# Two more pairs of up-projection tiles by seven products, with part of the operand work on GpSimd

## The chip, the cores and the metric

One core of a Trainium2 chip runs the kernel. Its engines have a queue of instructions each and wait for each other by semaphores: TensorE (PE; its weight loads are shown as PEld), VectorE (DVE), ScalarE (ACT), GpSimd (POOL) and SyncE (SP), which here only issues DMAs. The metric is the device time of one execution in microseconds (us): the median of the runs of a kernel. One further execution is profiled; the trace and its page are of that one.

## The reference, cut to what matters

The reference is one step of a decoder layer for 512 prompt positions and 8 samples of 4 positions, 544 rows in all: a mixer (recurrent branch, windowed attention, gates, output projection), and then a feed-forward network with a short convolution. The change lies in the second half:

```python
x = x + _rmsnorm(m, norm_mix_post[l])
u = _rmsnorm(x, norm_ffn_pre[l]) @ w_up              # 1024 -> 8192 columns
u, conv_state = _causal_dwconv(u, ffn_prev, ...)     # width 3 over positions
val, gate = jnp.split(u, 2, axis=-1)
f = (gelu(gate) * val) @ w_down                      # 4096 -> 1024
x = x + _rmsnorm(f, norm_ffn_post[l])
```

Everything is float32.

## The kernel before, in words

**Products.** Each float32 operand is split into a high part (a rounded copy, by ACT) and a low part (the operand less the high part, by DVE), and a product of two operands is three matmul passes: high by high, high by low, low by high. The up projection's 64 tiles of 128 columns are taken as 32 pairs: tile j of the values with tile 32 + j of the gates. The 544 rows are two halves of 272 (a = 0 and a = 1), and the 1024 rows of the weights two halves of 512 (u = 0 and u = 1). A "product" (`product`, L1522) is one half of the weights of a tile against one half of the rows: 4 blocks of 128 by three passes, 12 matmuls of 272 columns.

**Three ways for a pair.** Pairs 0 to 3 (`early`, L1372) are done plainly, 8 products each, first all 16 products of the first half of the rows, then all 16 of the second half. Pairs 4 and 5 (`PLAIN = 6`) are plain too, 8 products each, both halves of the rows together. Pairs 6 to 31 are done by a seven-product scheme (`pair`, L1640): the products a11, a12, p2, p3, p1, p4, a22 with the operands b11, b21, t2, t3, t1, b22, t4 (the table `XOF`). The weights of p2, p3, p1 and p4 are sums of quarters of the pair's two tiles, the operands t1 to t4 are sums of quarters of the normalised rows, and what the products give is added and subtracted again on the way out of PSUM (`taken`, `u4_c22`, `c11`, `c12`, `c21`; their copies `e` lie in the pool "parts", 5 buffers).

**Raw weights.** A tile of `w_up` is loaded by SP as 512 KB into one of 5 buffers ("raw"), in the order of use; a buffer is free again when the last split of its contents is done. A pair by eight products needs two raw tiles (`raw_up__...` of j and of 32 + j); a pair by seven products needs three, since the tile j is loaded a second time (`raw_up_s`) as the place in which the sums for p2 and p4 are made. `sums` (L1457) makes them in two parts: part 0 is one add by DVE, p3 = the second copy of tile j + the tile 32 + j; part 1 is one add by DVE in the tile 32 + j and two adding DMAs issued by GpSimd, the second of which waits for the first.

**Units, and how far ahead they are split.** A unit is what one (high, low) pair of split weights serves: for plain tiles two products, for the seven-product scheme one, for the down projection two halves. The list `units` has the 16 units of the early pairs first (0 to 15), in the order of the 16 products of the first half. `ahead(n)` (L1487) puts into the queues the loads up to unit n + 10, the high parts (ACT) and the low parts (DVE) up to n, and then every `sums` whose place has come: part 0 of a pair when n + 1 reaches the index of its p2 in the list less 4, part 1 one later (`SUMS = (4, 3)`, L1484 and L1499). While the 16 early products of the first half are written out, the product number k (from 0) calls `ahead(k + 5)`, up to 16; the first four of the second half call `ahead` with 17, 18, 19 and 20; after that the place moves with each unit used.

**Order.** The queues of PE, ACT and DVE in this stretch are written out by hand: instructions run in the order in which the program names them. A product is followed by a slot (`slot`, L1591): first what is due of earlier tiles (copies out of PSUM, the taps of the convolution, gelu and gate product: `tap`, `glu`), then `ahead`, then the generators that run beside the products (in the early products of the first half `ahead` comes after the generators). GpSimd's and SP's queues are put in order by a planner.

**The normalised rows.** `norm_chain(1, ...)` (L1232) runs beside the products, half a tick (one slot) for each `yield 0.5`. It makes the second half of the normalised rows: in slots 12 and 13 the tiles `h2t` and their splits b12 and b22, which product 16 and product 17 are the first to use; in slots 14 and 15 it forms t2 and the sum that becomes t1 in `h2f`; in 16 and 17 the sums that become t4 (two adds by DVE, 544 columns each); in 18 and 19 the high and the low part of t2; in 20 and 21 the sums that become t3 (two subtractions by DVE in `h2t`). Then it rests for `TX = 4` ticks (8 slots) and splits t3, t1 and t4 in slots 30 to 40, the high part and two slots later the low part, all low parts by DVE. The tiles `h2t` lie in a pool that is given up when the first tile of "parts" or "psums" (where the raw p3 of a pair lies) is asked for; the new pools lie over it.

**Down halves.** `plan` (L1372 to L1394) puts the halves of the down projection (12 matmuls of 256 or 288 columns) in between, once the pairs that they need are through: for plain pairs after the last product of a tile, two for a pair; for pairs by seven products after the products that `LAST_PLACES` names, by default four.

Of the kernel before, what the change touches and what calls it, by code (L numbers as in the profile page):

```python
# [11 lines left out]
F32 = mybir.dt.float32  # L12
F32R = mybir.dt.float32r
AF = mybir.ActivationFunctionType
ALU = mybir.AluOpType
AX = mybir.AxisListType

P = 128
# [40 lines left out]
HP = 150  # L59
NSTART = (1, 0.5)  # L60
EARLY = 4
PLAIN = 6
FB = (0.5,)
LASTS = 6
HELD = 5
TY = 1
TX = 4
DNS = 5
LAST_PLACES = {29: ('p3', 'p1', 'a22'), 30: ('p3', 'p1', 'a22'), 31: ('p1', 'a22')}
FIRST = 5  # L70
ATTN = (8, 10, 12, 14, 16, 18, 20, 22, 24, 26, 29, 32, 35, 38, 40, 42)
SAMPLE = (41, 46)
# [49 lines left out]
def hawk_step(ctx, tc, I, O):  # L122
    nc = tc.nc
    act, dve, pool, pe = nc.scalar, nc.vector, nc.gpsimd, nc.tensor
# [16 lines left out]
    def S(name, dt=F32):  # L141
        return sp.tile([P, SLOT], dt, tag="s", name=name)

    def T(name, dt=F32):
        return tp.tile([P, FLAT + 4], dt, tag="t", name=name)
# [13 lines left out]
    def f32(ap):  # L159
        return ap.bitcast(F32)  # L160
# [4 lines left out]
    def sub(out, a, b):  # L165
        dve.tensor_tensor(out=out, in0=a, in1=b, op=ALU.subtract)  # L166
# [4 lines left out]
    def add(out, a, b):  # L171
        dve.tensor_tensor(out=out, in0=a, in1=b, op=ALU.add)  # L172
# [984 lines left out]
    def total(accs, n, nm):  # L1157

        ps = PX("pst_" + nm)
        for z, acc in enumerate(accs):  # L1160
            mm(ps[:, :n], ones, acc[:, :n], z == 0, z == len(accs) - 1)
        return ps

    def root_table(ps, n, nm):

        y, w = (T(f"{x}_{nm}")[:, :n] for x in ("ry", "rw"))
        act.activation(y, ps[:, :n], AF.Abs_reciprocal_sqrt, scale=1.0 / D, bias=epst)
        act.activation(w, y, AF.Square, scale=1.0 / 32.0)
        return y, w
# [30 lines left out]
    def part_pool(which):  # L1200

        if not parts:
            trans.close()
            parts["e"] = ctx.enter_context(tc.tile_pool(name="parts", bufs=E_BUFS))
            parts["p"] = ctx.enter_context(tc.tile_pool(name="psums", bufs=2))
        return parts[which]
# [6 lines left out]
    def operand(nm, k, j):  # L1213

        if (nm, k // 2) not in B:
            B[nm, k // 2] = [S(f"{nm}{x}{k // 2}", F32R) for x in "HL"]
        return B[nm, k // 2][j][:, (k % 2) * HN:(k % 2 + 1) * HN]

    def operand2(nm, k2, j):

        operand(nm, 2 * k2, j)
        return B[nm, k2][j][:, 0:2 * HN]
# [9 lines left out]
    def norm_chain(a, acc):  # L1232
        lo, hi = HALF2[a]
        n = hi - lo
        with tc.high_priority(offset=HP):
            ps = total([acc], n, f"m{a}")
        yield YS[a]
        with tc.high_priority(offset=HP):
            yw = root_table(ps, n, f"m{a}")
            if a:  # L1240
                yield 0.5
            rep = root_newton(ps, n, *yw)
            acc2 = T(f"accx{a}")
            sq = {}

            def x1_(c):
                return x1[c][:, lo:hi]

            for c in range(0 if a else 8):
                m_ = mt[c][:, lo:hi]  # L1250
                stt(m_, m_, pvn[:, G_POST + c:G_POST + c + 1], rep[:, :n], ALU.mult, ALU.mult)
                pool.tensor_tensor(out=x1_(c), in0=x1_(c), in1=m_, op=ALU.add)
                sq_sum(acc2, x1_(c), n, c == 0, f"x{a}_{c}")
            for g in range(6 if a else 0):
                for c in range(2 * g, 2 * g + 2) if g < 4 else ():
                    m_ = mt[c][:, lo:hi]
                    stt(m_, m_, pvn[:, G_POST + c:G_POST + c + 1], rep[:, :n], ALU.mult, ALU.mult)
                    pool.tensor_tensor(out=x1_(c), in0=x1_(c), in1=m_, op=ALU.add)
                for c in range(2 * g - 3, 2 * g - 1) if 1 <= g < 6 else ():
                    if 0 <= c < 8:  # L1260
                        sq[c] = acc2 if c == 0 else T(f"sq_x{a}_{c}")
                        act.activation(sq[c][:, :n], x1_(c), AF.Square)
                for c in ((), (), (), (), (1, 2, 3), (4, 5, 6, 7))[g]:
                    add(acc2[:, :n], acc2[:, :n], sq[c][:, :n])
                yield 0.5
        yield NORM_TICKS[a]
        with tc.high_priority(offset=HP):
            ps = total([acc2], n, f"f{a}")
        yield YS[a]
        with tc.high_priority(offset=HP):  # L1270
            yw = root_table(ps, n, f"f{a}")
            if a:
                yield 0.5
            rep = root_newton(ps, n, *yw)

            def normed(c, dst):
                stt(dst, x1[c][:, lo:hi], pvn[:, G_FPRE + c:G_FPRE + c + 1], rep[:, :n], ALU.mult, ALU.mult)

            def first(k2):
                return h2f[k2][:, 0:2 * HN]  # L1280

            if a == 0:
                for k2 in range(5):
                    if k2 < 4:
                        for c in (2 * k2, 2 * k2 + 1):
                            normed(c, h2_half0(c))
                        act.activation(operand2(("b11", "b21")[k2 // 2], k2 % 2, 0), first(k2), AF.Copy)
                    if k2:
                        o = [operand2(("b11", "b21")[(k2 - 1) // 2], (k2 - 1) % 2, j) for j in range(2)]
                        sub(o[1], first(k2 - 1), f32(o[0]))  # L1290
                return
            n2 = {}

            def second(k2):
                return n2[k2]

            def high(nm, src):
                for k in range(2):
                    act.activation(operand2(nm, k, 0), src(k), AF.Copy)

            def low(nm, src):
                for k in range(2):
                    sub(operand2(nm, k, 1), src(k), f32(operand2(nm, k, 0)))

            for k2 in range(5):
                if k2 < 4:
                    n2[k2] = npool.tile([P, 2 * HN], F32, name=f"h2t{k2}")
                    for z in range(2):
                        normed(2 * k2 + z, n2[k2][:, z * HN:(z + 1) * HN])
                    act.activation(operand2(("b12", "b22")[k2 // 2], k2 % 2, 0), n2[k2], AF.Copy)  # L1310
                if k2:
                    o = [operand2(("b12", "b22")[(k2 - 1) // 2], (k2 - 1) % 2, j) for j in range(2)]
                    sub(o[1], n2[k2 - 1], f32(o[0]))
                if k2 in (2, 4):
                    yield 0.5
            for c in range(8):
                nc.sync.dma_start(out=x1d[c], in_=x1[c][:, 0:NT])
            t2 = [T(f"t2_{k}")[:, 0:2 * HN] for k in range(2)]
            for k in range(2):
                sub(first(k), first(k), second(k))  # L1320
                stt(t2[k], first(k), -1.0, second(2 + k), ALU.mult, ALU.subtract)
                yield 0.5
            for k in range(2):
                add(first(2 + k), first(2 + k), t2[k])
                yield 0.5
            high("t2", lambda k: t2[k])
            yield 0.5
            low("t2", lambda k: t2[k])
            yield 0.5
            for k in range(2):  # L1330
                sub(second(k), second(k), second(2 + k))
                yield 0.5
            yield TX
            for nm, src in (("t3", second), ("t1", first), ("t4", lambda k: first(2 + k))):
                high(nm, src)
                yield TY
                low(nm, src)
                yield TY

    def out_done(c, acc):  # L1340
# [36 lines left out]
    for p_ in range(EARLY, 32):  # L1377
        if p_ < PLAIN:
            todo_ = [("q", j, u, a) for j in (p_, 32 + p_) for u in range(2) for a in range(2)]
            places = [x for x in todo_ if x[2] == x[3] == 1]  # L1380
        else:
            todo_ = [("s", p_, nm) for nm in (XOF if p_ < 31 else ENDS)]
            places = [x for x in todo_ if x[2] in LAST_PLACES.get(p_, ("a12", "p3", "p1", "a22"))]
        for x in todo_:
# [15 lines left out]
    raws, usplit, used = {}, {}, [0, 0, 0]  # L1400
# [56 lines left out]
    def sums(p_, part):  # L1457
        w = {nm: source(("s", p_, nm)) for nm in ("p1", "p2", "p4", "a22")}
        if part == 0:
            raws["p3", p_] = part_pool("p").tile([P, 4, P], F32, tag="p", name=f"p3_{p_}")  # L1460
            add(raws["p3", p_], w["p2"], w["p1"])
        else:
            add(w["p1"], w["p1"], w["a22"])
            pool.dma_start(out=w["p2"], in_=w["p1"], accum_op=ALU.add)
            pool.dma_start(out=w["p4"], in_=w["p2"], accum_op=ALU.add)  # L1465
# [532 lines left out]
```

## Time and profile before

| what | before |
|---|---|
| median of 3 runs | 974.34 us (974.23 to 974.61) |
| the profiled execution, its own time | 973.95 us |
| its span | 972.2 us |
| PE busy | 963.0 us, 99% of the span, 7634 matmuls |
| DVE busy | 756.3 us, 78% |
| ACT busy | 553.9 us, 57% |
| POOL busy | 167.9 us, 17% |
| granted PE clock | 0.999 |

The profile's time axis starts with the span; the execution's own time is 1.75 us more than the span. In rows of the timeline the columns are start, length in us, engine, line, operation, what is written and read, how many instructions are merged, and in brackets how long the engine idled before and for whom. Lengths of neighbouring instructions overlap a little: 128x512 DVE operations of 0.69 us start 0.60 us apart when they are back to back. In rows of stretches (windows), the columns are the length of the stretch, the busy time and instructions of each engine, the granted PE clock, the share of the 16 DMA engines and GB/s.

### The profile page before, as it was taken

What the parts mean: (1) busy time and instruction counts of PE and PEld (TensorE: products, weight loads), DVE (VectorE), ACT (ScalarE), POOL (GpSimd) and SP (SyncE); (2) the same over time, 40 slices, a digit from 0 to 9 for tenths busy, and PEclk for the clock granted to TensorE, in tenths of its full rate; (3) what the DMA queues carried; (4) which work ended last, traced back from release to release, by engine and by line L of the source; (5) the groups of instructions that cost most, each with busy time, mean ns of one, the idle gap of its engine ahead of it and who ended that gap; (6) DMA issues with size and microseconds to landing.
All of it is one profiled execution on the core that took longest, in us unless ns stands there. A gap on an engine that the chain in (4) does not pass through costs nothing.

```text
span 972.2 us, 20023 instructions
## 1 busy us (share of the span) xinstructions
PE 963.0 (99%) x7634; PEld 955.2 (98%) x7634; DVE 756.3 (78%) x1599; ACT 553.9 (57%) x1349; POOL 167.9 (17%) x282
## 2 busy tenths in 40 slices
PE   9999999999999999999999999999999999999997
PEld 8999999999999999999999999999999999999996
DVE  5777888857858555599967888787888888888875
ACT  6544443467476425566767665655555555656653
POOL 2242000003406330230010111111011101020024
PEclk9999999999999999999999999999999999999999
DMA  7775535532334547135157575857576766668612
GB/s 229 236 213 180 151 89 147 162 93 87 108 110 128 179 115 189 52 121 186 45 117 182 128 198 123 192 130 181 136 181 157 171 155 156 170 145 219 201 31 92
DMA packets 234203, 143.07 MB, mean 147 GB/s; under 512 B 25012, under 2 KB 218940, under 8 KB 234076
## 3 DMA queue, kind: packets, MB, share of 16 engines
q1 hardware_dynamic: 224300, 120.21, 41.8%
q0 software_dynamic: 9696, 19.42, 11.8%
q10 hardware_dynamic: 112, 2.17, 0.6%
q8 instruction: 60, 0.98, 0.4%
q14 instruction: 35, 0.29, 0.1%
HBM read 115.59 MB, written 15.17 MB: 134 GB/s over the span
## 4 chain that ended last, share of the span: by engine, by line
PE 94%; DVE 3%; ACT 1%; issue 0%; DMA 0%; POOL 0%; SPq 0%; DVEq 0%; ACTq 0%; POOLq 0%
PE pmin L163 20%; PE pmdn L163 19%; PE pux L1527 16%; PE puy L1527 8%; PE pq L1527 6%; PE pmlo L163 5%; PE pmao L163 5%; PE pmout L163 4%; PE puz L1527 4%; PE pg L163 1%; PE pvp L163 1%; PE psc L163 1%; PE ptok L163 1%; DVE wl_e L166 0%; DMA pt<-pd 0%
## 5 line engine op out<-in xcount | busy, mean ns | idle before, releaser
L163 PE MATMUL pmin<-hH,wh_in 128*128 128x256 f32 (+1 forms) x568 | 164.0, 291 | 0.0
L163 PE MATMUL pmin<-hL,wh_in 128*128 128x256 f32 (+1 forms) x568 | 162.4, 288 | 0.0
L163 PE MATMUL pmin<-hH,wl_in 128*128 128x256 f32 (+1 forms) x568 | 159.1, 288 | 0.0
L163 PE MATMUL pmdn<-fH,wh_dn 128*128 128x256 f32 (+1 forms) x448 | 129.2, 288 | 0.0
L163 PE MATMUL pmdn<-fH,wl_dn 128*128 128x256 f32 (+1 forms) x448 | 129.0, 288 | 0.0
L163 PE MATMUL pmdn<-fL,wh_dn 128*128 128x256 f32 (+1 forms) x448 | 128.9, 288 | 0.0
L163 PEld LDWEIGHTS pmin<-hH,wh_in 128*128 128x128 f32 x568 | 107.2, 189 | 1.2 <-issue 1.0
L163 PEld LDWEIGHTS pmin<-hL,wh_in 128*128 128x128 f32 x568 | 107.2, 189 | 0.1
L163 PEld LDWEIGHTS pmin<-hH,wl_in 128*128 128x128 f32 x568 | 104.7, 188 | 0.2 <-issue 0.2
L175 DVE SCALAR_TENSOR_TENSOR uc<-u,fv,uc 128x560 f32<-128x560 f32 x128 | 102.0, 797 | 1.7 <-ACT uc L1558 1.1
L163 PEld LDWEIGHTS pmdn<-fH,wl_dn 128*128 128x128 f32 x448 | 84.4, 188 | 0.0
L163 PEld LDWEIGHTS pmdn<-fL,wh_dn 128*128 128x128 f32 x448 | 84.3, 188 | 0.1
L163 PEld LDWEIGHTS pmdn<-fH,wh_dn 128*128 128x128 f32 x448 | 84.2, 188 | 0.1
L1655 ACT COPY u<-pux 128x272 f32<-128x272 f32 x52 | 20.1, 387 | 86.0 <-PE pux L1527 86.0
L166 DVE TENSOR_TENSOR u<-puy,u 128x240 f32<-128x240 f32 (+2 forms) x78 | 24.6, 344 | 49.6 <-PE puy L1527 32.5
L172 DVE TENSOR_TENSOR ft<-ft,pmdn 128x256 f32<-128x256 f32 (+1 forms) x104 | 45.1, 434 | 16.7 <-PE pmdn L163 16.7
L281 ACT ACTIVATE wh_in<-raw_in 128x512 fp32r<-128x512 f32 x70 | 42.2, 625 | 19.0 <-issue 10.6
L288 DVE TENSOR_TENSOR wl_in<-raw_in,wh_in 128x512 fp32r<-128x512 f32 x70 | 47.8, 693 | 1.0 <-ACT wh_in L281 1.0
L1558 ACT ACTIVATE uc<-u,fv 128x560 f32<-128x560 f32 x64 | 48.2, 755 | 0.0
L779 ACT ACTIVATE s<-s,st 128x256 f32<-128x256 f32 (+1 forms) x32 | 15.2, 475 | 53.0 <-DVE st L776 42.5
L166 DVE TENSOR_TENSOR wl_dn<-raw_dn,wh_dn 128x512 fp32r<-128x512 f32 x56 | 38.3, 685 | 3.6 <-ACT wh_dn L1476 3.6
L1465 POOL DMA_DIRECT2D raw_up_s<-raw_up_s x26 | 22.4, 861 | 93.2 <-DMA raw_up_s<-raw_up__11237 5.5
(743 smaller groups left out, 3374.9 us busy)
## 6 DMA issues: line engine op xcount, KB each, us to landing
raw_in<-in_w_in_dram SPq DMA_DIRECT2D x35, 512.0 KB
raw_dn<-in_w_down_dram SPq DMA_DIRECT2D x56, 256.0 KB
raw_up_s<-in_w_up_dram SPq DMA_DIRECT2D x25, 512.0 KB
raw_up_s<-raw_up_s POOLq DMA_DIRECT2D x26, 256.0 KB, 4.3
raw_ao<-in_w_attn_o_dram SPq DMA_DIRECT2D x8, 512.0 KB
raw_lo<-in_w_lru_o_dram SPq DMA_DIRECT2D x8, 512.0 KB
raw_out<-in_w_out_dram SPq DMA_DIRECT2D x8, 512.0 KB
pd<-pb SPq DMA_DIRECT2D x12, 256.0 KB
```

The costliest lines, as they stand in the source:

```text
L163: pe.matmul(out, l, r, start=start, stop=stop)
L166: dve.tensor_tensor(out=out, in0=a, in1=b, op=ALU.subtract)
L172: dve.tensor_tensor(out=out, in0=a, in1=b, op=ALU.add)
L175: dve.scalar_tensor_tensor(out=out, in0=a, scalar=s_, in1=b, op0=op0, op1=op1)
L281: act.activation(hl[0], raw, AF.Copy)
L288: (eng or dve).tensor_tensor(out=hl[1], in0=raw, in1=f32(hl[0]), op=ALU.subtract)
L779: act.activation(s3[:, j, :], s3[:, j, :], AF.Exp, bias=ng[:, j:j + 1], accum_out=sm[:, j:j + 1])
L1465: pool.dma_start(out=w["p4"], in_=w["p2"], accum_op=ALU.add)
L1527: pe.matmul(ps[:, :HN], w, x, start=start and k == 0 and i == 0, stop=stop and k == 3 and i == 2, skip_group_check=True)
L1558: act.activation(yt[j][:, 0:FLATU], u[:, 0:FLATU], AF.Copy, scale=fv[:, j:j + 1])
L1655: act.copy(e[nm_], z)
```

## The change

Pairs 4 and 5 are no longer plain but done by the seven-product scheme, with two down halves each as before (after p1 and a22). The raw p3 of pair 4 is put into a general slot, not into the pool "psums". In `norm_chain` the two subtractions for t3 and the two adds for t4 go from DVE to GpSimd and stand in slot 16; t2 is split in slots 17 and 18; the rest is half a tick; then t3, t4 and t1 are split in this order in slots 19 to 29, the low parts of t3 and t4 (two instructions each) by GpSimd and that of t1 by DVE.

```diff
-PLAIN = 6
+PLAIN = 4
...
-TX = 4
+TX = 0.5
...
-LAST_PLACES = {29: ('p3', 'p1', 'a22'), 30: ('p3', 'p1', 'a22'), 31: ('p1', 'a22')}
+LAST_PLACES = {4: ('p1', 'a22'), 5: ('p1', 'a22'), 29: ('p3', 'p1', 'a22'), 30: ('p3', 'p1', 'a22'), 31: ('p1', 'a22')}
...
-            def low(nm, src):
+            def low(nm, src, eng=dve):
                 for k in range(2):
-                    sub(operand2(nm, k, 1), src(k), f32(operand2(nm, k, 0)))
+                    eng.tensor_tensor(out=operand2(nm, k, 1), in0=src(k), in1=f32(operand2(nm, k, 0)), op=ALU.subtract)
...
             for k in range(2):
-                add(first(2 + k), first(2 + k), t2[k])
-                yield 0.5
+                pool.tensor_tensor(out=second(k), in0=second(k), in1=second(2 + k), op=ALU.subtract)
+            for k in range(2):
+                pool.tensor_tensor(out=first(2 + k), in0=first(2 + k), in1=t2[k], op=ALU.add)
+            yield 0.5
             high("t2", lambda k: t2[k])
             yield 0.5
             low("t2", lambda k: t2[k])
-            yield 0.5
-            for k in range(2):
-                sub(second(k), second(k), second(2 + k))
-                yield 0.5
             yield TX
-            for nm, src in (("t3", second), ("t1", first), ("t4", lambda k: first(2 + k))):
+            for nm, src, eng in (("t3", second, pool), ("t4", lambda k: first(2 + k), pool), ("t1", first, dve)):
                 high(nm, src)
                 yield TY
-                low(nm, src)
+                low(nm, src, eng)
                 yield TY
...
         if part == 0:
-            raws["p3", p_] = part_pool("p").tile([P, 4, P], F32, tag="p", name=f"p3_{p_}")
+            if p_ == PLAIN:
+                raws["p3", p_] = S(f"p3_{p_}")[:, 0:512].rearrange("p (k n) -> p k n", k=4)
+            else:
+                raws["p3", p_] = part_pool("p").tile([P, 4, P], F32, tag="p", name=f"p3_{p_}")
             add(raws["p3", p_], w["p2"], w["p1"])
```

## The prediction

> **What bounds the kernel now.** I read the page's busy table first, then the chain that ended last, then stretches around the edit, then the queues in order of time.
>
> ```profile
> PE 963.0 (99%) x7634; PEld 955.2 (98%) x7634; DVE 756.3 (78%) x1599; ACT 553.9 (57%) x1349; POOL 167.9 (17%) x282
> 417.40:436.30 18.90, 18.40 (x140) 17.58 (x139) 17.54 (x33) 13.15 (x29) 7.71 (x8) 1.00 0.43 137
> 436.30:447.00 10.70, 10.70 (x88) 10.70 (x87) 10.43 (x21) 6.15 (x13) 0.00 (x0) 1.00 0.96 301
> 447.00:468.00 21.00, 21.00 (x169) 21.00 (x169) 19.11 (x39) 15.80 (x52) 0.00 (x0) 1.00 0.28 85
> 468.00:498.00 30.00, 30.00 (x242) 30.00 (x241) 23.75 (x42) 21.25 (x59) 1.81 (x2) 1.00 0.35 90
> 414.32 1.72 DVE h2f L175 x4
> 436.32 49.67 PE pq L1527 x396
> 485.99 4.43 PE pmdn L163 x36
> 490.42 6.04 PE pq L1527 x48
> ```
>
> TensorE sets the time: it is busy 99%, and the chain runs through it without a break from 436.32 on. So a removed product is worth its length, and a microsecond for which TensorE is made to wait is lost. But where the edit lies DVE is nearly as full: busy 17.54 of 18.90 us, 10.43 of 10.70, 19.11 of 21.00. The last links of the chain that aren't TensorE are DVE's normalised rows (414.32). The engine that the edit loads is the one without room.
>
> The chain gives the clock of what follows. 396 matmuls are 33 products in 49.67 us, 1.505 us each. They end with the twelfth plain product of pairs 4 and 5, so they are products 11 to 43 of the stretch; product k starts at 436.32 + (k - 11) x 1.505: product 16, the first to use b12, at 443.85, product 17 (b22) at 445.35, product 32 (the first of pair 4) at 467.93.
>
> **1. What is removed.** Two pairs by 7 instead of 8 products: -2 x 1.505 = **-3.0 us**, whole, as nothing else fills TensorE. The number of down halves stays (two a pair before, two after).
>
> **2. The sums of pair 4 move up, into DVE's fullest place.** This is the step that I think decides.
>
> ```profile
> 481.27 0.69 DVE L166 TENSOR_TENSOR wl_dn<-raw_dn,wh_dn 128x512 fp32r<-128x512 f32 x1
> 481.88 0.68 DVE L172 TENSOR_TENSOR p<-raw_up_s,raw_up__6410 128x512 f32<-128x512 f32 x1
> 484.35 0.69 DVE L172 TENSOR_TENSOR raw_up__6410<-raw_up__6410 128x512 f32<-128x512 f32 x1
> 435.46 0.68 DVE L166 TENSOR_TENSOR wl_e<-raw_up__5779,wh_e 128x512 fp32r<-128x512 f32 x1
> 436.06 0.68 DVE L166 TENSOR_TENSOR wl_e<-raw_up__5883,wh_e 128x512 fp32r<-128x512 f32 x1
> 436.66 0.69 DVE L166 TENSOR_TENSOR wl_e<-raw_up__5918,wh_e 128x512 fp32r<-128x512 f32 x1
> 437.92 0.69 DVE L166 TENSOR_TENSOR wl_e<-raw_up__5918,wh_e 128x512 fp32r<-128x512 f32 x1
> 438.53 0.43 DVE L175 SCALAR_TENSOR_TENSOR rw_f<-pst_f,rw_f 128x272 f32<-128x272 f32 x1
> 444.11 1.53 DVE L166 TENSOR_TENSOR b22L<-h2t,b22H 128x544 fp32r<-128x544 f32 x2
> 433.72 0.38 SPq L1440 DMA_DIRECT2D raw_up__6065<-in_w_up_dram  x1
> 436.17 0.38 SPq L1440 DMA_DIRECT2D raw_up__6115<-in_w_up_dram  x1
> 436.64 1.51 SPq L1317 DMA_DIRECT2D x1d<-x  x2
> ```
>
> Before, the first pair by seven products is pair 6, and its p2 is unit 28; the rule n + 1 = 28 - 4 puts part 0 of its sums behind the low part of unit 22, and there it is, 481.88 behind 481.27. After, p2 of pair 4 is unit 18, so part 0 comes at n = 13, behind the low part of unit 12 (436.06), and part 1 one low part later. At 436.66 DVE thus comes to an add that reads the second copy of tile 4. This copy is the eleventh raw tile; there are five buffers, so it takes that of the sixth, which is free when unit 11 is split (435.46 + 0.68). Before, the eleventh load is raw_up__6115, issued at 436.17, right behind that. So the add is reached half a microsecond after its load is issued. How long does a load take?
>
> ```profile
> 875.64 0.37 SPq L1440 DMA_DIRECT2D raw_up_s<-in_w_up_dram  x1
> 882.61 0.69 DVE L172 TENSOR_TENSOR p<-raw_up_s,raw_up__12376 128x512 f32<-128x512 f32 x1 [0.94 <-DMA raw_up_s<-in_w_up_dram]
> 485.64 0.94 POOL L1464 DMA_DIRECT2D raw_up_s<-raw_up__6410  x1 [53.81 <-DVE raw_up__6410 L172]
> 489.26 0.87 POOL L1465 DMA_DIRECT2D raw_up_s<-raw_up_s  x1 [2.68 <-DMA raw_up_s<-raw_up__6410]
> ```
>
> Pair 30's same add waited for its load and started 6.97 us after the issue. The lower end is the 256 KB transfer that GpSimd waited for, 3.62 us. So the copy lands between 439.8 and 443.1. In between: the DMA engines are 96% busy here at 301 GB/s, with raw_up__6065 (512 KB) and an x1d store (272 KB) queued before; with the copy's own 512 KB that is 1.33 MB or 4.4 us from 436.3, and the two stores of 436.64 share in it. I take 441.2.
>
> Behind the waiting add in DVE's queue stand the low parts of units 13 to 15, and rw_f, h2t, b12 and b22, which TensorE needs at products 13 to 17. All come later by the wait (441.2 - 436.66 = 4.5) and the two adds (0.60 each, back to back): 5.75 us. The room: the second b22 low part ends at 445.64, and product 17 needs it in its eighth matmul, at 445.35 + 7 x 0.125 = 446.23; so 0.6 is hidden. **+5.1 us** (3.75 to 7.05 for the two ends).
>
> **3. DVE in slots 14 to 36.** Edits that go together: four operand sums and t3's and t4's low parts leave DVE, t1's low part comes ahead of pair 4, pair 5's p3 add comes into slot 19, and from slot 33 every product needs a low part of its own.
>
> ```profile
> 448.36 0.72 DVE L172 TENSOR_TENSOR h2f<-h2f,t 128x544 f32<-128x544 f32 x1
> 452.05 1.35 DVE L166 TENSOR_TENSOR t2L<-t,t2H 128x544 fp32r<-128x544 f32 x2
> 454.88 1.35 DVE L166 TENSOR_TENSOR h2t<-h2t,h2t 128x544 f32<-128x544 f32 x2
> 469.62 0.91 DVE L175 SCALAR_TENSOR_TENSOR z<-uc,fv,uc 128x512 f32<-128x512 f32 x2 [0.83 <-ACT uc L1569]
> 470.45 1.64 DVE L175 SCALAR_TENSOR_TENSOR uc<-u,fv,uc 128x560 f32<-128x560 f32 x2
> 473.27 0.72 DVE L166 TENSOR_TENSOR fL<-z,fH 128x544 fp32r<-128x544 f32 x1
> 477.21 1.35 DVE L166 TENSOR_TENSOR t1L<-h2f,t1H 128x544 fp32r<-128x544 f32 x2
> 424.12 7.71 POOL L1258 TENSOR_TENSOR x<-x,mt 128x272 f32<-128x272 f32 x8 [17.48 <-DVE mt L175]
> 424.37 1.08 DVE L166 TENSOR_TENSOR wl_e<-raw_up__5773,wh_e 128x512 fp32r<-128x512 f32 x1
> 426.18 1.18 DVE L166 TENSOR_TENSOR wl_e<-raw_up__5775,wh_e 128x512 fp32r<-128x512 f32 x1
> 299.58 1.42 POOL L1014 TENSOR_TENSOR xc<-xc,lt 128x568 f32<-128x568 f32 x1
> 299.65 1.95 DVE L175 SCALAR_TENSOR_TENSOR lt<-lt,th 128x568 f32<-128x568 f32 x1 [0.25 <-POOL lt L1005]
> 291.06 0.73 DVE L175 SCALAR_TENSOR_TENSOR lt<-lt,th 128x568 f32<-128x568 f32 x1
> ```
>
> GpSimd isn't free for DVE: while it adds (424.12), a low part takes 1.08 to 1.18 us instead of 0.69, about 0.48 more; at 299.65 a DVE operation that starts just after a GpSimd one takes 1.95 instead of 0.73, 1.22 more. A 568-column GpSimd operation takes 1.42 us, so the eight moved ones (544 columns) are some 11 us of GpSimd. It idles from 431.83 to 485.64, so its own queue has room, but DVE pays 0 to 1.22 for each, while doing one itself costs it 0.65. I take 0.48, the row with GpSimd back to back beside low parts: 3.8 us.
>
> DVE's lateness at slot 32, behind the start of product 32: before 468.79 - 467.93 = 0.9. To it come 0.6 from step 2 (5.75 less 5.1), -2.6 for the two adds and two subtractions, +1.3 for t1, +0.6 for pair 5's add, 3.8 beside GpSimd; -1.6 as two gaps of 0.8 before z close; and a second wait: pair 5's copy takes the buffer that unit 17's low part frees, and DVE then has only t2's and two more low parts (2.6 us) before that add, against 3.6 at the least for a load: +1.0. Sum 4.0 us.
>
> The allowance: the low part for p1 of pair 4 (product 36) stands in slot 33, behind z 0.83, two taps 1.55 (start to start) and pair 5's second add 0.60, and takes 0.69: 3.7 us. TensorE needs it 4 x 1.505 + 0.25 = 6.3 us after product 32 starts, so 2.6 us of lateness are free and 1.4 are a stall. Then slot 34 has two taps, fL, a subtraction of about 0.4 and the next low part, 3.25 us against one product of 1.5: 1.75 more. **+3.1 us**. The ends: 0 without any cost beside GpSimd and without the second wait (lateness 0.8); 9.0 at 1.22 for each operation (lateness 9.9).
>
> [...]
>
> **4. At nothing.** ACT's six more high parts (0.6 us each) and p-copies lie in its idle share (15.8 of 21.0 busy); a late high part would show as in step 3. t3, t1 and t4 are needed at products 35, 36 and 38 and split 7 to 14 slots sooner. Pair 5's p3 and the copies `e` lie over `h2t`, whose last readers, on GpSimd, stand in slots 16 to 21; the first `e` is written in slot 33, and if p3 in slot 19 had to wait for them, that would lie in the second wait. The two more loads and four adding DMAs find the DMA engines at 28 to 35% after 447. Everything after pair 5 is as before, only shifted.
>
> **The sum.** -3.0 + 5.1 + 3.1 = +5.2 us. From the profiled execution's 973.95 (span 972.2, 1.75 around it) that is 979.15; it lies 0.4 below the median of the runs, 974.34. Forecast 979.5 us.
>
> **The rivals.**
>
> *Faster: the add doesn't wait.* Place: the p3 add behind unit 12's low part. If the copy has landed when DVE gets there, step 2 costs only the two adds less the room, 0.6, and with step 3 at its lower end the time is 974.34 - 3.0 + 0.6 = 971.9. It is faster as long as the copy lands before 439.1 (wait 2.4, with the two adds less the room 3.0). Against it: the buffer is freed at 436.14, and no load in these rows lands in 2.9 us. For it: I infer the order of buffers from before's loads, and a planner hands them out. 12%.
>
> *A short wait and no second stall.* Landing at 439.8 and step 3 at 0: 975.0, up to about 977. For it: DVE loses work in slots 16 to 21, and the gaps before z can take more of it. 22%.
>
> *GpSimd blocks DVE whole.* 1.22 for each of eight operations: step 3 becomes 9.0, the time 985.4. For it: the row of 299.65, and DVE's dense queue after slot 14. Against: the rows at 424 to 427 show under half. 16%.
>
> *The forecast's case*, 977 to 983: 50%.
>
> **Range and chances.** 973.0 to 985.0 leaves out the faster case and about half of the heavy one; the likeliest case's own range is 977 to 983. A measurement here tells 0.2% (1.95 us) from no change. Slower by more: the forecast, the heavy case and a third of the short wait, 0.73. Within: the rest of the short wait, 0.15. Faster: 0.12.
>
> **What would show it.** DVE's p3 add of pair 4 near 436.7 to 441 with a bracket naming the DMA of the second copy, and TensorE waiting for low parts near products 13 to 17: step 2; without that wait it is wrong. The chain of waits leaving TensorE there for DVE and the load. p1 and p4 of pair 4 waiting for wl_s_p: step 3. DVE operations of 0.7 us shown with 1.2 to 2 beside GpSimd's eight: the third rival. TensorE's busy matmuls down by 24: step 1. If there's no idle on TensorE between 436 and 500, the forecast is wrong and 971.3 stands.

## The result, and the profile after

| what | before | after |
|---|---|---|
| median | 974.34 us (974.23 to 974.61) | 989.83 us (989.11 to 990.40) |
| the profiled execution, its own time | 973.95 us | 989.23 us |
| its span | 972.2 us | 987.3 us |
| matmuls | 7634 | 7610 |
| granted PE clock, mean | 0.999 | 0.990 |

The changed kernel is slower: ratio 1.0158, 95% interval 1.0144 to 1.0172. That is 15.5 us where 5.2 were forecast, and 989.8 lies above the range given (973.0 to 985.0).

The busy table of the page after, and four stretches of the changed kernel (columns as before: length, busy time of PE, PEld, DVE, ACT, POOL, PE clock, DMA share, GB/s):

```profile
PE 964.8 (98%) x7610; PEld 956.6 (97%) x7610; DVE 769.4 (78%) x1611; ACT 557.5 (56%) x1351; POOL 185.5 (19%) x294
```

```profile
436.30:447.00 10.70, 6.91 (x42) 6.69 (x41) 5.26 (x10) 1.81 (x4) 0.94 (x1) 0.78 0.56 174
447.00:468.00 21.00, 21.00 (x162) 21.00 (x161) 20.80 (x29) 12.55 (x32) 11.48 (x7) 0.95 0.49 130
468.00:498.00 30.00, 20.67 (x154) 20.44 (x152) 27.22 (x50) 22.07 (x63) 5.16 (x4) 0.83 0.25 63
498.00:531.00 33.00, 33.00 (x265) 33.00 (x264) 26.12 (x51) 22.81 (x58) 3.39 (x4) 1.00 0.75 186
```

TensorE has 24 matmuls less, and yet 1.8 us more busy time: its matmuls became longer. It idles in two of these stretches, 3.8 us in the first and 9.3 in the third, where it was full before, and in both the granted clock is well under 1. From 498 on TensorE is full again, as before: the first product of pair 6 starts at 512.58 instead of 497.87, 14.7 us later, and the last matmul 15.0 us later. So nearly the whole loss lies between 436 and 498.

**The first wait.** In order of time, SP's load of the second copy of tile 4, DVE around the add that needs it, and TensorE behind it:

```profile
436.31 0.38 SPq L1438 DMA_DIRECT2D raw_up_s<-in_w_up_dram  x1
...
436.20 0.68 DVE L166 TENSOR_TENSOR wl_e<-raw_up__5883,wh_e 128x512 fp32r<-128x512 f32 x1
442.18 0.69 DVE L172 TENSOR_TENSOR p<-raw_up_s,raw_up__6065 128x512 f32<-128x512 f32 x1 [5.29 <-DMA raw_up_s<-in_w_up_dram]
...
443.53 0.59 PE L1528 MATMUL pq<-b11H,wl_e 128*128 128x272 f32 x1 [3.79 <-DVE wl_e L166]
443.92 0.43 PE L1528 MATMUL pq<-b11H,wh_e 128*128 128x272 f32 x1
444.15 0.43 PE L1528 MATMUL pq<-b11L,wh_e 128*128 128x272 f32 x1
```

The add stands behind unit 12's low part and waits 5.29 us for a load that was issued 0.1 us after that low part began. From the load's issue to the add are 5.9 us. TensorE runs dry and waits 3.79 us for the next low part. Then its matmuls start 0.23 us apart instead of 0.125. The granted clock in stretches of 2 us says why:

```profile
440.00:442.00 2.00, 0.00 (x0) 0.00 (x0) 0.00 (x0) 0.00 (x0) 0.00 (x0) 1.00 1.05 364
442.00:444.00 2.00, 0.47 (x2) 0.47 (x3) 1.82 (x4) 0.00 (x0) 0.00 (x0) 0.59 0.17 64
446.00:448.00 2.00, 2.00 (x10) 2.00 (x10) 1.89 (x6) 0.67 (x2) 0.00 (x0) 0.50 0.58 133
448.00:450.00 2.00, 2.00 (x13) 2.00 (x13) 2.00 (x5) 1.20 (x2) 0.00 (x0) 0.70 1.15 259
```

The clock falls to half at about 442.4 (0.59 over two microseconds) and is full again at about 449.2 (0.70). TensorE works at half speed for 5.7 us of that and loses 2.8. Product 16 starts at 450.42; in the kernel before it started at 443.66 (the prediction's nominal time was 443.85). Less 0.14 us that were there ahead of the edit, TensorE has lost 6.6 us by then. (The expectations below say 6.4, reckoned from the nominal time.)

**The second wait.** ACT and DVE around slot 32, and TensorE's third product of pair 4:

```profile
483.89 0.76 ACT L1570 ACTIVATE uc<-uc,fv 128x560 f32<-128x560 f32 x1 [1.51 <-DVE uc L175]
484.69 0.92 DVE L175 SCALAR_TENSOR_TENSOR z<-uc,fv,uc 128x512 f32<-128x512 f32 x2 [0.83 <-ACT uc L1570]
486.51 0.36 ACT L1656 COPY e<-pux 128x272 f32<-128x272 f32 x1
486.93 0.59 PE L1528 MATMUL pux<-t2H,wh_s_p 128*128 128x272 f32 x1 [9.33 <-ACT e L1656]
```

p2 of pair 4 writes the PSUM bank (the buffer for products, `pux` in the rows) that a11 filled, and may do so when ACT has copied a11 out as `e`. That product ended some 10 us before. But the copy stands in ACT's queue behind the gelu of an early pair (483.89), and the gelu waits for DVE's taps; the copy runs only at 486.51, after them. The chain of waits goes the same way, over DVE's operations and ACT's gelu, and comes back to TensorE at `486.93`, with 12 matmuls in 3.09 us instead of 1.51: half the clock again, until about 490.2, which costs 1.6 us.

**Why DVE is so late there.** GpSimd's moved operations and what DVE does beside them:

```profile
453.18 1.75 POOL L1324 TENSOR_TENSOR h2t<-h2t,h2t 128x544 f32<-128x544 f32 x1 [1.43 <-ACT wh_s_a L1477]
456.69 1.85 POOL L1324 TENSOR_TENSOR h2t<-h2t,h2t 128x544 f32<-128x544 f32 x1
461.12 3.46 POOL L1303 TENSOR_TENSOR t3L<-h2t,t3H 128x544 fp32r<-128x544 f32 x2 [0.79 <-ACT t3H L1299]
...
453.62 1.89 DVE L166 TENSOR_TENSOR h2f<-h2f,h2t 128x544 f32<-128x544 f32 x1
457.25 1.85 DVE L166 TENSOR_TENSOR wl_s_a<-raw_up__6014,wh_s_a 128x512 fp32r<-128x512 f32 x1
459.03 1.85 DVE L166 TENSOR_TENSOR wl_s_a<-raw_up__6014,wh_s_a 128x512 fp32r<-128x512 f32 x1
465.04 0.68 DVE L166 TENSOR_TENSOR wl_s_p<-p,wh_s_p 128x512 fp32r<-128x512 f32 x1
```

A low part that takes 0.68 us by itself (465.04) takes 1.85 beside GpSimd (457.25, 459.03): 1.17 more, and the two engines go on in step, one DVE operation and one GpSimd operation in 1.8 us (GpSimd's own rows: 1.75, 1.85, 3.46 for two). Over all eight the DVE operations beside them take 1.0 to 1.2 us more each. DVE's lateness at slot 32 (the moment at which it falls idle before z, less the start of a11 of pair 4) is 484.69 - 0.83 - 474.43 = 9.4 us; 4.0 were forecast.

**The account.** From the profiled 973.95: -3.0 for two products, +3.8 and +9.3 of waits, +2.8 and +1.6 of half clock gives 988.5, of a measured 989.23. Of the remaining 0.7 us, 0.1 was there ahead of 436, and 0.3 comes little by little between pair 6 and the last matmul, without a wait; the rest has no place in the rows.

### The profile page after: what moved, and what is told of

Same layout as the page of the kernel before. It is cut to its first block, busy times and chain, and to the rows that moved or that the text cites. A ratio compares the mean times of both kernels' runs of the same rounds, so it can differ in the third digit from the quotient of the medians.

```text
span 987.3 us, 20034 instructions
## 1 busy us (share of the span) xinstructions
PE 964.8 (98%) x7610; PEld 956.6 (97%) x7610; DVE 769.4 (78%) x1611; ACT 557.5 (56%) x1351; POOL 185.5 (19%) x294
## 4 chain that ended last, share of the span: by engine, by line
PE 88%; DVE 6%; issue 2%; ACT 2%; DMA 1%; POOL 0%; SPq 0%; DVEq 0%; ACTq 0%; POOLq 0%
PE pmin L163 20%; PE pmdn L163 17%; PE pux L1528 17%; PE puy L1528 8%; PE pmlo L163 5%; PE pmao L163 5%; PE pmout L163 4%; PE puz L1528 4%; PE pg L163 1%; DVE uc L175 1%; PE pvp L163 1%; PE psc L163 1%; PE ptok L163 1%; DVE wl_e L166 1%; DMA raw_up_s<-in_w_up_dram 1%
## 5 line engine op out<-in xcount | busy, mean ns | idle before, releaser
L1528 PE MATMUL pux<-t2H,wh_s_p 128*128 128x272 f32 x112 | 32.9, 294 | 9.3 <-ACT e L1656 9.3
```

The source lines that it names most:

```text
L1528: pe.matmul(ps[:, :HN], w, x, start=start and k == 0 and i == 0, stop=stop and k == 3 and i == 2, skip_group_check=True)
```

## The experiments

All medians, intervals and ratios are against runs of the kernel before on the same chip (974.2 to 974.3 us).

### 1. The add of pair 4 reads the first copy of tile 4

```diff
-            add(raws["p3", p_], w["p2"], w["p1"])
+            add(raws["p3", p_], source(("s", p_, "a11")), w["p1"])
```

> The add that makes p3 reads the first copy of tile j (same numbers, loaded two tiles earlier) instead of the second; nothing else changes. Theory A (two separate waits: first DVE for the load, then p2 of pair 4 for its copy e, which is as late as DVE is at slot 32): the add then waits for tile 36 alone, issued at 433.86, and starts near 439 instead of 442.2; TensorE loses 2 to 3 us there instead of 6.4, the second wait stays at 9 to 10 us: 985 to 987 us. Rival B (DVE has too much work between 436 and 496, and TensorE gets it in the end wherever it shows): the second wait grows by what the first loses, 989 to 990 us.

Measured: 987.27 us (987.0 to 987.78), ratio 1.0134 [1.0119, 1.0149]. In order of time, the add on DVE, and then TensorE's waits from 380 to 560 (total, times, longest):

```profile
438.88 0.69 DVE L172 TENSOR_TENSOR p<-raw_up__6014,raw_up__6065 128x512 f32<-128x512 f32 x1 [1.93 <-DMA raw_up__6065<-in_w_up_dram]
```

```profile
PE pux L1528 <- ACT e L1656: 10.0, 1, 10.0
PE pq L1528 <- DVE b12L L166: 0.8, 2, 0.4
PE pq L1528 <- DVE wl_e L166: 0.4, 1, 0.4
PE pq L1528 <- DVE b22L L166: 0.4, 1, 0.4
```

The add now waits 1.9 us for tile 36 instead of 5.3 for the second copy, and TensorE's first wait is down to four pieces of 0.4. So the second copy's load was the cause of the first wait. But 2.6 us are won and not 3.8 + 2.8: the four pieces remain, the second wait grows from 9.3 to 10.0, and more matmuls run at half clock behind it (20 start 0.23 us apart, from 484.4 to 488.7, against 11 from 487.3 to 489.8). The time lies just over the first theory's range; the wait of 10 us is as it said, and its rival's 989 to 990 did not come.

### 2. GpSimd's part alone, without the pairs

```diff
-PLAIN = 4
+PLAIN = 6
-LAST_PLACES = {4: ('p1', 'a22'), 5: ('p1', 'a22'), 29: ...
+LAST_PLACES = {29: ...
```

> Only the operand part of the change (four sums and four low parts on GpSimd, t3, t4, t1 split sooner), pairs 4 and 5 plain as before. Theory A: DVE's two-input operations take 1.2 us more beside GpSimd's eight as in the changed kernel, some 9 us in all, but pair 4 needs no copy e and no low part of its own for each product, so TensorE waits for nothing: 974.0 to 975.5 us. Rival B: DVE's loss comes through to TensorE, 977 to 982 us.

Measured: 978.82 us (977.39 to 980.25), ratio 1.0047 [1.0030, 1.0064]. TensorE's waits:

```profile
PE pq L1528 <- DVE wl_q L166: 1.6, 1, 1.6
PE pq L1528 <- ACT wh_q L1477: 0.6, 1, 0.6
```

The eight operations on GpSimd, sooner, cost 4.5 us by themselves, with both pairs plain: 2.2 us of waits near 480 to 483, and 1.7 of half clock behind them (3.4 us at half, from 483.5 on); 0.6 is what two breaks cost beyond the waits (see the seventh experiment). The second theory holds: DVE had room before, but not enough for the blocking. The four executions lie far apart, and so do their mean clocks (977.39 us at 0.999, 980.25 at 0.996); the figures here are those of the profiled one, 978.79.

### 3. Pair 5 alone by seven products, GpSimd's part kept

```diff
-PLAIN = 4
+PLAIN = 5
-LAST_PLACES = {4: ('p1', 'a22'), 5: ('p1', 'a22'), 29: ...
+LAST_PLACES = {5: ('p1', 'a22'), 29: ...
```

> As the change, but pair 4 stays plain and only pair 5 goes by seven products. Its sums are due in slot 16, behind b12 and b22, and its second copy takes a buffer freed earlier. Theory A: no first wait; DVE has eight more products (12 us) to get level before p2 of pair 5 asks for its copy e, and its lateness of some 9 us is gone: one product saved, 972.8 to 974 us. Rival B: the lateness is still there, 977 to 981 us.

Measured: 981.73 us (981.64 to 981.87), ratio 1.0077 [1.0062, 1.0092]. TensorE's waits:

```profile
PE pux L1528 <- DVE wl_s_a L166: 1.6, 1, 1.6
PE pq L1528 <- ACT u L1622: 1.2, 2, 0.9
PE pux L1528 <- ACT wh_s_a L1477: 1.1, 1, 1.1
PE pux L1528 <- ACT e L1656: 1.0, 1, 1.0
```

Waits of 4.9 us in five pieces, on DVE and on ACT alike. The second theory is right that the lateness is still there, the time 0.7 us over its range. Pair 4 accounts for 8.1 of the 15.5 us, but half of the loss stays without it.

### 4. The sums of pair 4 behind the normalised rows

```diff
+SHIFT = 4
-                  if key[0] == "s" and key[2] == "p2")
+                  if key[0] == "s" and key[2] == "p2" and key[1] != PLAIN)
-            add(raws["p3", p_], w["p2"], w["p1"])
+            add(raws["p3", p_], source(("s", p_, "a11")), w["p1"])
-            slot(s_ <= AHEAD, 0 if s_ == AHEAD else 1)
+            if s_ == 1:
+                sums(PLAIN, 0)
+                sums(PLAIN, 1)
+            slot(SHIFT < s_ <= SHIFT + AHEAD, 0 if s_ == SHIFT + AHEAD else 1)
```

> As the change, but both sums of pair 4 stand in slot 16, behind b12 and b22, p3 reads the first copy, and units 16 to 19 are split four slots later. Theory A: no wait at products 13 to 17, so 6.4 us come back; DVE's lateness at slot 32 and with it p2's wait stay near 9 us plus 1.5 at the lower clock: 982 to 984 us. If the lateness comes mostly from the first wait, p2's wait shrinks to 3 to 5 us: 976 to 978. Rival B: 988 to 990 us.

Measured: 985.85 us (985.25 to 986.32), ratio 1.0119 [1.0104, 1.0134]. TensorE's waits:

```profile
PE pux L1529 <- ACT e L1657: 10.1, 1, 10.1
PE puz L1529 <- ACT u L1623: 1.1, 1, 1.1
```

The first wait is gone (6.6 us of it and its clock), but only 4.0 us are won, less than either reckoning of the first theory: a new wait of 1.1 us stands ahead of the second, which stays at 10 us. So the second wait is no consequence of the first; DVE is as late for other reasons.

### 5. Six of GpSimd's eight operations back on DVE

t3's two low parts stay on GpSimd.

```diff
-                pool.tensor_tensor(out=second(k), in0=second(k), in1=second(2 + k), op=ALU.subtract)
+                sub(second(k), second(k), second(2 + k))
-                pool.tensor_tensor(out=first(2 + k), in0=first(2 + k), in1=t2[k], op=ALU.add)
+                add(first(2 + k), first(2 + k), t2[k])
-            for nm, src, eng in (("t3", second, pool), ("t4", lambda k: first(2 + k), pool), ("t1", first, dve)):
+            for nm, src, eng in (("t3", second, pool), ("t4", lambda k: first(2 + k), dve), ("t1", first, dve)):
```

> The changed kernel with six of GpSimd's eight operations back on DVE (the four operand sums and t4's two low parts; t3's two low parts stay). A, GpSimd's operations block DVE for their whole length, about 1.2 us each as the rows of the changed kernel show, where DVE needs 0.65 for one: DVE is 6 x 0.55 = 3.3 us sooner at the first copy e of pair 4, and TensorE's second wait falls from 9.3 to about 6: 986 to 987 us. B, what delays DVE is its own work (low parts, taps, adds) and GpSimd costs it little: DVE has 6 x 0.65 = 3.9 us more to do, and the time goes up to 991 to 994.

Measured: 986.62 us (986.33 to 986.88), ratio 1.0126 [1.0110, 1.0142]: 3.2 us faster than the changed kernel, for a forecast of 3.3. The wait on the copy e:

```profile
PE pux L1528 <- ACT e L1656: 6.7, 1, 6.7
```

DVE with six operations more to do is 2.6 us sooner (its lateness at slot 32 is 481.73 - 0.83 - 474.10 = 6.8 us instead of 9.4). The blocking theory holds in sign and size; the rival, that DVE's own work is what delays it, would have made it slower.

### 6. The early pairs' gelu three slots later

```diff
-            chain += [(3, glu, p_, 0), (4, glu, p_, 1), (5, glu, p_, 2), (6, glu, p_, 3)]
+            g = 3 if j in early else 0
+            chain += [(3 + g, glu, p_, 0), (4 + g, glu, p_, 1), (5 + g, glu, p_, 2), (6 + g, glu, p_, 3)]
```

> The changed kernel with gelu, gate product and split of the early pairs three slots later, so that ACT's copy e of pair 4's a11 does not stand behind a gelu that waits for DVE. A, it is DVE's lateness as a whole that TensorE meets: the wait moves from the copy e to the low parts of p3 and p1, and little is won (986 to 989 us; 2.5 us at most, DVE's three gaps of 0.83 before z). B, the wait is one of ACT's order: the copy e is written in time, TensorE's second wait falls to under 3 us, and the time to 980 to 984.

Measured: 985.34 us (984.9 to 985.8), ratio 1.0112 [1.0096, 1.0128]. The second wait falls from 9.3 to 5.3 us, still on the copy e. DVE is now busy 29.25 of the 30 us from 468 to 498 (27.22 before this edit), so the gaps in which it waited for gelu are used. The result lies between the two theories. More is won than DVE's three gaps (2.5 us), so I take it that ACT's order has a share; it isn't the whole, and one run does not part the two.

### 7. What a wait of TensorE costs

The kernel before, with ACT's copy of a11 repeated in three pairs far from the edit:

```diff
-            act.copy(e[nm_], z)
+            for _ in range({12: 9, 16: 20, 20: 38}.get(p_, 1) if nm_ == "e1" else 1):
+                act.copy(e[nm_], z)
```

> The kernel before, with ACT's copy e of a11 repeated 9 times in pair 12, 20 times in pair 16 and 38 times in pair 20, so that TensorE waits once in each, with nothing else added. It measures what an idle stretch of TensorE costs beyond its own length. At some 0.25 to 0.3 us for a copy the stalls are about 1, 4 and 9 us. A, a stall costs its length: the sum of the three waits equals the time lost, and matmuls behind it run 0.125 us apart. B, after a stall of about 4 us or more the granted clock stays at half for some us, as behind the waits of the changed kernel: 2 to 3 us more for each of the two long ones, none for the short one, so some 5 us more than the waits.

Measured: 998.52 us (997.82 to 999.27), 24.2 us more than before. The copies follow each other every 0.42 us (the 0.25 to 0.3 above were my estimate), and TensorE's waits were 0.89, 5.48 and 12.98 us, 19.4 in all. In the profiled execution (997.82, 23.9 more than before) 4.5 us more were lost than TensorE waited. The first wait, the clock behind it, and the clock around the second wait, which ends at 674.81:

```profile
602.86 0.39 PE L1527 MATMUL pux<-t2H,wh_s_p 128*128 128x272 f32 x1 [0.89 <-ACT e L1656]
603.09 0.29 PE L1527 MATMUL pux<-t2L,wh_s_p 128*128 128x272 f32 x1
604.00:606.00 2.00, 2.00 (x19) 2.00 (x18) 2.00 (x4) 1.32 (x3) 0.00 (x0) 1.00 0.04 8
670.00:672.00 2.00, 0.00 (x0) 0.00 (x0) 0.00 (x0) 1.84 (x6) 0.00 (x0) 0.83 0.00 0
676.00:678.00 2.00, 2.00 (x11) 2.00 (x10) 2.00 (x4) 0.07 (x1) 0.00 (x0) 0.50 0.00 0
678.00:680.00 2.00, 2.00 (x17) 2.00 (x17) 2.00 (x5) 2.00 (x5) 0.08 (x1) 0.96 0.02 7
```

The second theory holds. Behind 0.89 us the clock stays full. In the second wait it falls at about 671.3 and is full again at about 678.1, 3.3 us after TensorE resumed; behind the third it was half for another 4.4 us. At half speed that is 1.6 + 2.2 = 3.8 of the 4.5 us. Even at full clock a break costs some 0.3 us beyond its bracket: behind the first wait the matmuls stand 1.18 us later than they would, for 0.89 of waiting. A matmul is shown with 0.29 us and the next starts 0.125 later, so a bracket, counted from the end of the one before, leaves out 0.16; and the first one behind the wait is followed after 0.23.

### 8. Pair 5 alone, all operand work on DVE

The kernel before with

```diff
-PLAIN = 6
+PLAIN = 5
-LAST_PLACES = {29: ...
+LAST_PLACES = {5: ('p1', 'a22'), 29: ...
+            if p_ == PLAIN:
+                raws["p3", p_] = S(f"p3_{p_}")[:, 0:512].rearrange("p (k n) -> p k n", k=4)
+            else:
                 raws["p3", p_] = part_pool("p").tile([P, 4, P], F32, tag="p", name=f"p3_{p_}")
-            add(raws["p3", p_], w["p2"], w["p1"])
+            add(raws["p3", p_], source(("s", p_, "a11")), w["p1"])
```

> The kernel before with pair 5 alone by seven products, all operand work on DVE at its old place (rest of 4 ticks), the raw p3 of pair 5 in a general slot and its add reading the first copy of tile 5. A, without GpSimd's blocking DVE keeps up and the removed product is worth its length: 974.3 - 1.5 = 972.8 us. B, the pair's own work (three more low parts, two sums, the copies) is what the full stretch of DVE cannot take, and the loss of 9 us of the changed kernel with pair 5 alone is DVE's own: 976 to 981.

Measured: 974.52 us (974.23 to 974.78), ratio 1.0003 [0.9994, 1.0012]: no difference. Against the third experiment it is 7.2 us faster, with the same pairs and products; what differs is GpSimd's part, its earlier places, and which copy the sum reads. Neither theory's number came out. One wait is left, 1.1 us on the copy e of pair 5, and with the 0.3 of a break it takes back most of the 1.5 us of the product saved.

### 9 and 10. Two pairs, mended, with GpSimd's part and without it

The ninth is the changed kernel with the edits of the fourth and the sixth experiment and

```diff
-            result(f)
+            if p_ == PLAIN and nm == "a11":
+                todo.setdefault(turn[0], []).insert(1, f)
+            else:
+                result(f)
```

The tenth is the ninth with `norm_chain` as in the kernel before but for `TX = 0.5`, so that all eight operations are DVE's; the raw p3 of pair 5 lies in a general slot too.

> The changed kernel, with GpSimd's eight operations kept and three mends at once: the sums of pair 4 four slots later and from the first copy of tile 4 (as in the fourth experiment), the early pairs' gelu three slots later (as in the sixth), and the copy e of pair 4's a11 put into ACT's queue one slot sooner. A, these are separate causes: the single gains of 4.0 and 4.5 us add up, and the copy e gives up to 1 more: 980 to 982 us. B, both only move the same lateness of DVE about, which TensorE then meets at the low parts: 984 to 986.

> As the run before it, with all eight operations back on DVE at the places of the kernel before (only the rest is the short one). A, GpSimd's lock is a cause of its own even where nothing else delays DVE: 3 to 4 us sooner than the run before it, about 977 to 978; the fifth experiment showed 3.2 for six. B, with the mends the lock lies in room that DVE has again, and the two runs are within 1 us.

Measured: the ninth 980.64 us (980.44 to 980.86), ratio 1.0066 [1.0052, 1.0080]; the tenth 976.18 us (975.8 to 978.25), ratio 1.0024 [1.0014, 1.0035]. TensorE's waits in the ninth, and in the tenth:

```profile
PE pux L1529 <- ACT e L1658: 4.5, 1, 4.5
PE puy L1529 <- DVE u L167: 1.3, 1, 1.3
```

```profile
PE puy L1531 <- DVE u L167: 1.3, 1, 1.3
PE puw L1531 <- DVE wl_s_p L167: 1.3, 1, 1.3
PE pux L1531 <- ACT u L1660: 0.8, 1, 0.8
```

By GpSimd's lock the expectation means what the rows show, a DVE operation of 0.68 us that takes 1.85 beside GpSimd; that a lock is behind it was not shown. The gains of the fourth and sixth experiments add up (989.83 - 4.0 - 4.5 = 981.3, measured 980.64), so the first wait and what the later gelu mends are separate causes; the copy put sooner is worth 0.7 us at most. The first theory holds in both, though the tenth lies 0.8 us under its range: GpSimd's part costs another 4.5 us where the others are gone, and without it the long wait on the copy e is gone. The tenth still stands 1.9 us over the kernel before: in the profiled execution (977.2) 3.4 us of short waits, their breaks and a stretch of half clock (3.4 us from about 480.7 on) take more than the 3.0 us of two products. Its seven executions go from 975.8 us at a mean clock of 1.000 to 978.25 at 0.996, so the stretch of half clock does not seem to come in each. I take it that pair 4 does not find the room on DVE; no run tries pair 4 alone.

### 11 and 12. Pair 5 alone, the copy sooner, the gelu later

The eleventh is the eighth with the copy e put into the queue one slot sooner (the edit shown above). The twelfth is that with the gelu three slots later for all of pairs 0 to 4 (`g = 3 if p_ < PLAIN else 0`).

> The eighth experiment (pair 5 alone by seven products, all operand work on DVE) with the copy e of pair 5's a11 put into ACT's queue one slot sooner, ahead of the tap and the high parts of that slot. A, the single wait of 1.1 us that was left comes from ACT's order: it goes, and the time is 973.0 to 973.5, under the 974.3 of the kernel before. B, it is lateness of the stretch: another wait takes its place and the time stays at 974.2 to 974.8.

> As the run before it, and the gelu, gate product and split of pairs 0 to 4 three slots later, so that nothing of ACT waits for DVE ahead of the copy e. A, as there: 972.8 to 973.3, the whole of the removed product. B, the delayed work now stands beside pair 5's own copies and low parts and makes a new wait: 974 to 976.

Measured: the eleventh 974.38 us (974.0 to 974.6), ratio 1.0002 [0.9993, 1.0011]; the twelfth 973.30 us (973.18 to 973.71), ratio 0.9991 [0.9982, 1.0000]. Sooner alone, the wait of 1.1 is broken into two of 0.6 and 0.4: another wait takes its place, as the second theory said. With the gelu later, TensorE has no wait left from 436 to 531:

```profile
468.00:498.00 30.00, 30.00 (x242) 30.00 (x241) 27.16 (x51) 24.37 (x64) 1.67 (x2) 1.00 0.37 98
```

Pair 6 then begins 1.3 us sooner than before (496.57 against 497.87), near the 1.5 of the product. The first theory of the twelfth holds. The end is only 0.75 us sooner in the trace: the lead melts little by little between pair 6 and 880 us, with the clock full (1.00 in the stretches from 498 to 900) and no wait, as it does by 0.3 us in the changed kernel; why stays open. Its highest run (973.71) lies under the lowest of the kernel before (973.73), but the interval ends at 1.0000 and 0.9 us is under the 0.2% that I call a difference: the best kernel of this study, by a little.

## Why the prediction was wrong

**Step 1, two products saved, -3.0 us: right.** 24 matmuls less; in the twelfth experiment one removed product moves pair 6 by 1.3 of 1.5 us.

**Step 2, the add waits for its load, +5.1 us: the mechanism right, the price short.** The add stands where it was put, its bracket names the load, and with the first copy (1) it shrinks to 1.9 us for another tile, with the sums four slots later (4) it goes. DVE waited 5.29 us where 4.5 were forecast, inside the bounds; the load took 5.9 us, between the rows of 3.6 and 7.0. TensorE's loss was 6.6 us at product 16: 3.8 us of waiting, which is less than the 5.1, and 2.8 at half speed, for which the sum had no term. By then the lateness of b12 and b22, in which I had put the price, was hidden, since TensorE itself had slowed down.

**Step 3, DVE in slots 14 to 36, +3.1 us: this step failed, in three ways.** *The cost beside GpSimd.* I took 0.48 us for each operation from the rows at 424 to 427. They stand beside GpSimd operations of 272 columns; the moved ones have 544, and cost 1.17. The other row of the prediction, 299.65 with 568 columns and 1.22 us, was the nearer one by size. With 0.7 us more for each of eight, my sum of 4.0 becomes 9.6; measured 9.4. That the two agree so closely is partly luck: the two gaps before z that were to close (-1.6) are still there (0.83, 0.82 and 0.83 us at 470.28, 477.93 and 484.69), and the second wait (+1.0) did not come. Experiments 5 and 10 confirm the price: 3.2 us for six, 4.5 for eight. *The place.* I expected p1 and p4 to wait for low parts, with 2.6 us of lateness free. TensorE met the lateness two products sooner, at p2, through ACT: the copy e stands behind a gelu that waits for DVE. Thus none of it was free, and the wait was 9.3 us, nearly the whole lateness, where 3.1 were forecast. *The clock*, 1.6 us more: the prediction put what TensorE loses behind a wait at nothing, without a reason.

**Step 4, at nothing: wrong for ACT.** I looked at ACT's idle share and not at its order. Busy 22.07 of 30.00 us from 468 to 498, ACT still held TensorE up for 9.3 us, as the copy that was needed stood behind a gelu that waited. Experiments 6 and 12 bear it out: a later gelu is worth 4.5 us in the changed kernel, of which up to 2.5 may be DVE's gaps, and 1.1 in the kernel with pair 5 alone. The loads and adding DMAs cost nothing that can be seen: pair 5's add (465.64) follows a low part (465.04) without a gap, and the DMA engines were 25 to 49% busy from 447 to 498.

**The rivals.** *GpSimd blocks DVE whole*, with 16%, had the right price, 1.22 us for an operation against 1.0 to 1.2 measured; its 985.4 us lacks 4.4. The half clock of both waits is 2.8 + 1.6 = 4.4, but that match is luck in part, as its waits were 5.1 and 9.0 against 3.8 and 9.3 measured. The faster case fell with the load's 5.9 us, the short wait with the load and the second wait. What was said would show the third rival, DVE operations of 0.7 us shown with 1.2 to 2, is what the rows show.

**What stays open.** Some 0.3 us of the account, and of the third experiment about 1: it lost 8.9 us against the 972.8 that one product saved would give, of which 4.9 are waits, some 1.7 half clock and some 1.4 the five breaks. How the second wait's 9.3 us divide between GpSimd's blocking, ACT's order and DVE's added work is shown only by the differences of runs (2.6 us of the wait by six operations, 4.0 by the gelu), not by one view.

## What to carry to other kernels

Before an operation goes from DVE to GpSimd, compare its price in a row of the same size: here each operation cost DVE 1.17 us where doing it cost 0.65, so "idle" GpSimd was dearer than busy DVE. For a stage that is added, follow each hand-over in the queue of every engine on the way, and ask which instruction ahead of it waits for the engine that is full; a busy share doesn't show that. And price a wait of TensorE of several microseconds at its length and then the half clock behind it, here 1.6 to 2.8 us more.

## What the runs showed of the hardware

The granted clock fell to half around waits of TensorE and stayed there for several microseconds: from 442.4 to 449.2 (6.8 us) at the first wait, from about 479.9 to 490.1 (10.2) at the second, from 671.3 to 678.1 (6.8) in the seventh experiment, and 3.4 us in the tenth (from about 480.7 to 484.0). In the tenth there is no single long wait. Two waits of 1.3 us lie around the fall with matmuls between them: from 477 to 481 TensorE was busy for 1.52 of 4.00 us, and the clock fell. A lone wait of 0.9 us (7) or 1.1 us (8) left it full.

```profile
477.00:478.00 1.00, 0.00 (x0) 0.00 (x0) 1.00 (x2) 0.00 (x0) 0.84 (x1) 1.00 0.00 0
478.00:479.00 1.00, 0.74 (x6) 0.75 (x7) 1.00 (x4) 0.00 (x0) 0.01 (x1) 1.00 0.49 90
479.00:480.00 1.00, 0.78 (x7) 0.56 (x5) 1.00 (x3) 0.94 (x2) 0.00 (x0) 1.00 1.15 156
480.00:481.00 1.00, 0.00 (x0) 0.00 (x0) 0.70 (x5) 1.00 (x4) 0.00 (x0) 0.83 0.74 180
481.00:482.00 1.00, 0.90 (x4) 0.90 (x5) 1.00 (x3) 0.97 (x5) 0.00 (x0) 0.50 1.12 338
```

These rows are of the tenth experiment. How much idle time brings the clock down, and what ends the half clock, no run here shows.

The second finding is the price of working side by side. Four DVE operations of the changed kernel that started 0.4 to 0.7 us behind a GpSimd operation of 544 columns took 1.77 to 1.89 us (0.68 to 0.72 by themselves), and each ended 0.55 to 0.6 us behind the end of that GpSimd operation. So both engines went on at about one operation in 1.8 us.

```profile
453.18 1.75 POOL L1324 TENSOR_TENSOR h2t<-h2t,h2t 128x544 f32<-128x544 f32 x1 [1.43 <-ACT wh_s_a L1477]
454.89 1.84 POOL L1326 TENSOR_TENSOR h2f<-h2f,t 128x544 f32<-128x544 f32 x1
456.69 1.85 POOL L1324 TENSOR_TENSOR h2t<-h2t,h2t 128x544 f32<-128x544 f32 x1
458.50 1.83 POOL L1326 TENSOR_TENSOR h2f<-h2f,t 128x544 f32<-128x544 f32 x1
453.62 1.89 DVE L166 TENSOR_TENSOR h2f<-h2f,h2t 128x544 f32<-128x544 f32 x1
455.55 1.77 DVE L175 SCALAR_TENSOR_TENSOR t<-h2f,h2t 128x544 f32<-128x544 f32 x1
457.25 1.85 DVE L166 TENSOR_TENSOR wl_s_a<-raw_up__6014,wh_s_a 128x512 fp32r<-128x512 f32 x1
459.03 1.85 DVE L166 TENSOR_TENSOR wl_s_a<-raw_up__6014,wh_s_a 128x512 fp32r<-128x512 f32 x1
```
